# One buffer and one transfer for both parts of a weight tile, its rest made by VectorE, and six buffers for the norms

## The chip, the core and the metric

One core of a Trainium2 chip runs the whole kernel: TensorE (PE) multiplies, VectorE (DVE), ScalarE (ACT) and GpSimd (POOL) do the elementwise work, SyncE (SP) issues almost all transfers. The metric is the time of one execution in microseconds (us), as the median of several runs.

## The reference

One layer of a hybrid encoder over 2048 tokens of width 1024, in float32. What matters here is its first third, the input projection and the mixers that read it:

```python
h = rms_norm(x, mix_norm_g[l])
proj = h @ w_in[l]                      # (2048, 1024) @ (1024, 3332)
pa, pb, pc = ...                        # columns of A, B, C
# A: chunked attention, B: forgetting attention: q and k are RMS-normed per head of 64
# C: RWKV-7 recurrence over its columns (r, k, v and three low-rank inputs)
x = x + concat([ya, yb, yc]) @ w_out[l]
x = x + conv_glu_ffn(rms_norm(x, ffn_norm_g[l]), w_up[l], conv_w[l], conv_b[l], w_down[l])
```

## The kernel before

Tokens lie along the free axis. The first phase walks over four blocks of 512 tokens. For each block it makes the projection by tiles of weights (26 tiles of 1024 rows by 128 columns, or halves of that depth by 256 or 260), the q and k norms (`qk_in`), the v rows (`v_in`), and three interleaved stages of the recurrence: `rwkv_front`, `rwkv_inverse` (a chain of 62 small VectorE instructions, tiles `tm` and `T`) and `rwkv_back`. The later phases (attention, output projection, feed-forward) are not touched.

To keep float32 accuracy, each operand is split in two: a high part rounded to the matmul's type (`hi`, a ScalarE copy) and the rest (`lo`, a subtraction on another engine), and each product is three matmuls: hi by hi, hi by lo, lo by hi. In a projection these are lines 268 to 270; line 270 is the one that reads the weight's `lo`.

`load_w` delivers a weight tile. In the first block it loads the raw tile into `wraw` (three buffers), makes `whi` on ScalarE and `wlo` on GpSimd (on VectorE for five tiles: the first one and the four of `v_in`), two buffers of each, and stores both parts in DRAM with two transfers (`whiD`, `wloD`). In the three later blocks it reloads both parts with two transfers, in two of three cases into `whi` and `wlo`, in the third into two `wraw` buffers.

Small tiles of 128 by 512 with the tag `fl` come from one pool of four buffers in rotation: the squares `sq`, the scales `rn`, the split outputs `qh` and `ql` of the q and k norms, which are stored to DRAM (`qkD`), the sums `acc` of the norm of the next block, and a few more. A buffer is used again when all that read it, a store too, have ended.

The code asks for a weave of these jobs; the framework then sets the order of the instructions on each engine when the program is built, and adds the waits. Each engine takes its own instructions strictly in that order, SP's transfers too.

Of the kernel before, what the change touches and what calls it, by code (L numbers as in the profile page):

```python
# [11 lines left out]
F32 = mybir.dt.float32  # L12
F32R = mybir.dt.float32r
# [15 lines left out]
LEV = {'acc': G_, 'w': G_, 'kka': V, 'kf': V, 'rk': V, 'n': V, 'l': V, 'ql': V, 'ak': G_, 'gn': V, 'kr': V, 'uv': S_, 'r': V, 'w_': V, 'y': V, 'dt': V, 'bp': V, 'qa': V}  # L29
NEED = (21, 9, 4, 0, 9, 20, 6, 59)  # L30
AHEAD = 3
XG = 4
BUFS = {"fr": 7, "bk": 4, "bp": 2, "fl": 4, "wraw": 3, "wspl": 2, "xt": 2, "pr": 3, "p2": 6, "vs": 1, "st": 4, "raw": 3, "yh": 5, "xr": 3, "tmp": 5, "wu": 4, "s4": 4, "hid": 4, "x4": 3, "vv": 1}
PACE = 1
KSTAT = 1
X0N = 1
# [11 lines left out]
DQ = lambda nc: nc.sync  # L48
PSB = {"m": 3, "f": 2, "b": 2}
PSM = {"m": "PQVSNBLq", "f": "TA", "b": "b"}  # L50
WB = (2, 0)
GAP = ((0, 0, 21, 0), (12, 0, 12, 0), (12, 0, 3, 0), (15, 0, 0, 0))
PARK = 3
QQ = lambda nc: nc.scalar
# [43 lines left out]
def trunk_kernel(ctx: ExitStack, tc: tile.TileContext, xT, w_in, pp, cst, cau, rel, relr, w2, a2, g2, w_out, w_up, w_down, out, dbg=None):  # L98
    nc = tc.nc
# [3 lines left out]
    def f(ap):  # L103
        return ap.bitcast(F32)
# [4 lines left out]
    dram = ctx.enter_context(tc.tile_pool(name="dram", bufs=1, space=DRAM))  # L109
# [32 lines left out]
    def split(hi, lo, src, hi_eng=None, lo_eng=None):  # L142
        (hi_eng or nc.scalar).copy(hi, src) if (hi_eng or nc.scalar) is nc.scalar else hi_eng.tensor_copy(out=hi, in_=src)  # L143
        (lo_eng or nc.vector).tensor_tensor(lo, src, f(hi), op=ALU.subtract)  # L144


    p1 = ExitStack()
    hTp = p1.enter_context(tc.tile_pool(name="hTp", bufs=1, side="right"))
    xtp = p1.enter_context(tc.tile_pool(name="xtp", bufs=1, side="right"))
    ws = p1.enter_context(tc.tile_pool(name="ws", bufs=1, side="right"))  # L150
    wl = p1.enter_context(tc.tile_pool(name="wl", bufs=1, side="right"))
    flp = p1.enter_context(tc.tile_pool(name="flp", bufs=BUFS["fl"], side="right"))
    sp = p1.enter_context(tc.tile_pool(name="sp", bufs=4))
# [81 lines left out]
        nc.vector.memset(S, 0.0)  # L235
        Ss.append(S)

    kept, turn = {}, [0]

    def load_w(r0, c0, w, n, lo_eng=None, raw=None, who="Q"):  # L240


        src = w_in[r0 : r0 + n * P, c0 : c0 + w]
        if (r0, c0) in kept:
            turn[0] = (turn[0] + 1) % 3
            if turn[0] == 0:
# [6 lines left out]
        if raw is None:
            raw = wl.tile([P, n, 1040 // n], F32, name="wraw", tag="wraw", bufs=BUFS["wraw"])
            nc.sync.dma_start(out=raw[:, :, 0:w], in_=src.rearrange("(k p) c -> p k c", p=P))
        hi, lo = (ws.tile([P, n, 1040 // n], F32R, name=m, tag=m, bufs=2) for m in ("whi", "wlo"))
        split(hi[:, :, 0:w], lo[:, :, 0:w], raw[:, :, 0:w], None, lo_eng or LEV['w'](nc))
        kept[r0, c0] = [dram.tile([P, n, w], F32, name=f"{m}{r0}_{c0}") for m in ("whiD", "wloD")]
        for t, d in zip((hi, lo), kept[r0, c0]):
            nc.sync.dma_start(out=d, in_=f(t[:, :, 0:w]))  # L260
        return hi, lo

    def project(hT, c0, raw=None, who="P"):

        hi, lo = load_w(0, c0, P, KT, raw and nc.vector, raw, who)
        ps = psm[who].tile([P, TB], F32, name="mm", tag="ps")
        for kt in range(KT):
            mm(ps, hi[:, kt, 0:P], hT[kt][:, 0, :], start=(kt == 0), stop=False)  # L268
# [573 lines left out]
    for b in range(NB):  # L842
# [3 lines left out]
        lo = {} if b else lo0  # L846
# [25 lines left out]
    p2 = ExitStack()  # L872
# [245 lines left out]
    for u, (n, qb) in enumerate(units):  # L1118
# [8 lines left out]
        k = 0  # L1127
# [58 lines left out]
    for b, (t0, n) in enumerate(BL):  # L1186
        done = Y
        for hf in range(2):
# [11 lines left out]
            for k in range(KT):  # L1200
# [3 lines left out]
                yh = yhp.tile([P, 2, HN], F32R, name="yh")[:, :, 0:n]  # L1204
# [24 lines left out]
            for ct in range(KT):  # L1229
                xt = Y[ct][:, cs]  # L1230
# [19 lines left out]
    s4 = p4.enter_context(tc.tile_pool(name="s4", bufs=BUFS["s4"]))  # L1250
# [6 lines left out]
    x4 = p4.enter_context(tc.tile_pool(name="x4", bufs=BUFS["x4"]))  # L1257
# [206 lines left out]
```

## Time and profile before

| | |
|---|---|
| median of 3 runs | 3266.54 us (3254.4 to 3267.34) |
| the profiled execution, its time | 3256.01 us |
| its span from first to last instruction | 3254.2 us |
| first phase, blocks 1 to 4 | to 343, 630, 915 and 1195 us |

The profiled execution is one of the quicker ones: 10.5 us below the median of the runs. The ends of the blocks are read from the first reload of weights (342.9 us) and from the repeating pattern behind it, to a few us. A row of a timeline gives start, duration, engine, line, operation, output and inputs, the count of merged instructions, and in brackets the idle time of that engine just ahead and what ended it. A row of windows gives the stretch and its length, the busy time of TensorE, its weight loads, VectorE, ScalarE and GpSimd with their counts of instructions, then TensorE's granted clock, the busy share of the DMA engines and what they moved in GB/s. A row of waits gives who waited for whom, the sum, the count and the longest. The granted clock of TensorE is 1.00 at 2.4 GHz and 0.50 at 1.2 GHz.

### The profile page before, as it was taken

How to read it: one execution, taken by the hardware profiler on the slowest of the kernel's cores; microseconds unless marked ns; L12 is line 12 of the kernel's file. 1: busy time of each engine (PE TensorE's matmuls, PEld its weight loads, DVE VectorE, ACT ScalarE, POOL GpSimd, SP SyncE). 2: the span in 40 equal slices, each digit the busy share in tenths (PEclk: the TensorE clock that was granted, in tenths of full speed). 3: DMA queues.
4: the chain of work that ended last, by engine and by line, in shares of the span. 5: the costliest groups of instructions: out<-in, count | busy, mean ns of one | idle time of the engine just before them, and what ended most of it. 6: DMA issues, size and time to landing. Idle time of an engine off the chain costs nothing.

```text
span 3254.2 us, 49317 instructions
## 1 busy us (share of the span) xinstructions
PE 3037.6 (93%) x17820; PEld 2650.9 (81%) x17820; DVE 2373.9 (73%) x4569; ACT 1399.3 (43%) x2610; POOL 1000.3 (31%) x949
## 2 busy tenths in 40 slices
PE   6888899999999979999999999999899999999999
PEld 4567777776777755667699899999799998899999
DVE  5666666766677645677644688889988889988886
ACT  5343444434444334578733333333333334333332
POOL 3221001001000020144433444444544444444442
PEclk8888899999999987999999999999999999999999
DMA  7555665655653565532224422222422222422221
GB/s 222 148 166 170 175 181 163 190 149 157 162 161 101 169 152 141 141 99 77 76 90 148 143 79 78 78 78 74 154 74 77 78 78 81 140 78 78 78 79 67
DMA packets 440228, 392.94 MB, mean 121 GB/s; under 512 B 138809, under 2 KB 365637, under 8 KB 438633
## 3 DMA queue, kind: packets, MB, share of 16 engines
q1 hardware_dynamic: 435056, 377.99, 39.7%
q0 software_dynamic: 2816, 8.39, 0.9%
q10 hardware_dynamic: 2112, 3.41, 0.5%
q8 instruction: 141, 2.31, 0.3%
q14 instruction: 103, 0.84, 0.1%
HBM read 304.65 MB, written 86.36 MB: 120 GB/s over the span
## 4 chain that ended last, share of the span: by engine, by line
PE 66%; DVE 18%; issue 5%; ACT 4%; DMA 4%; POOL 2%; SPq 1%; POOLq 0%; ACTq 0%; DVEq 0%
PE ps L1291 7%; PE ps L1290 7%; PE ps L1289 7%; PE ps L1337 4%; PE ps L1335 4%; PE ps L1336 4%; PE mm L268 3%; PE mm L270 3%; PE mm L269 3%; DVE T L523 2%; PE o L1061 2%; DVE tm L520 2%; DVE wu L144 2%; PE z L639 2%; PE ps L1197 2%
## 5 line engine op out<-in xcount | busy, mean ns | idle before, releaser
L1291 PE MATMUL ps<-B,wu 128*128 128x340 f32 (+1 forms) x1848 | 593.2, 321 | 20.0 <-DVE wu L144 20.0
L1290 PE MATMUL ps<-B,wu 128*128 128x340 f32 (+1 forms) x1848 | 592.0, 320 | 0.0
L1289 PE MATMUL ps<-B,wu 128*128 128x340 f32 (+1 forms) x1848 | 589.4, 319 | 2.5 <-ACT wu L143 1.7
L1291 PEld LDWEIGHTS ps<-B,wu 128*128 128x128 f32 x1848 | 348.0, 188 | 27.6 <-DVE wu L144 27.2
L1335 PE MATMUL ps<-hid,wd 128*128 128x340 f32 (+1 forms) x1056 | 342.1, 324 | 14.3 <-ACT wd L143 10.2
L1289 PEld LDWEIGHTS ps<-B,wu 128*128 128x128 f32 x1848 | 347.9, 188 | 3.2 <-ACT wu L143 2.0
L1290 PEld LDWEIGHTS ps<-B,wu 128*128 128x128 f32 x1848 | 348.6, 189 | 0.1
L1337 PE MATMUL ps<-hid,wd 128*128 128x340 f32 (+1 forms) x1056 | 339.9, 323 | 3.1 <-POOL wd L144 3.0
L1336 PE MATMUL ps<-hid,wd 128*128 128x340 f32 (+1 forms) x1056 | 339.9, 322 | 0.0
L144 DVE TENSOR_TENSOR wu<-S,wu 128x512 fp32r<-128x512 f32 x264 | 257.0, 978 | 74.7 <-ACT wu L143 74.7
L1338 DVE TENSOR_TENSOR acc<-acc,ps 128x340 f32<-128x340 f32 (+1 forms) x528 | 248.3, 503 | 52.9 <-PE ps L1337 52.2
L144 POOL TENSOR_TENSOR wd<-raw,wd 128x1024 fp32r<-128x1024 f32 x66 | 171.0, 2613 | 277.3 <-ACT wd L143 272.9
L268 PE MATMUL mm<-hT,whi 128*128 128x512 f32 x520 | 235.9, 454 | 18.0 <-ACT whi L143 12.8
L270 PE MATMUL mm<-hT,wlo 128*128 128x512 f32 x520 | 220.3, 424 | 10.4 <-POOL wlo L144 6.4
L143 ACT CAST wu<-S 128x512 fp32r<-128x512 f32 x264 | 163.1, 619 | 150.5 <-PE ps L1291 137.9
L269 PE MATMUL mm<-hT,whi 128*128 128x512 f32 x520 | 219.3, 422 | 4.9 <-DVE hT L144 3.9
L1335 PEld LDWEIGHTS ps<-hid,wd 128*128 128x128 f32 x1056 | 201.8, 191 | 18.0 <-ACT wd L143 11.0
L144 DVE TENSOR_TENSOR wu<-raw,wu 128x512 fp32r<-128x512 f32 x198 | 203.0, 1026 | 6.4 <-ACT wu L143 6.4
L1337 PEld LDWEIGHTS ps<-hid,wd 128*128 128x128 f32 x1056 | 200.2, 190 | 5.5 <-POOL wd L144 5.5
L1336 PEld LDWEIGHTS ps<-hid,wd 128*128 128x128 f32 x1056 | 201.2, 190 | 0.0
L143 ACT CAST wu<-raw 128x512 fp32r<-128x512 f32 x198 | 121.5, 620 | 165.3 <-PE ps L1291 147.4
L268 PEld LDWEIGHTS mm<-hT,whi 128*128 128x128 f32 x520 | 105.5, 203 | 49.5 <-ACT whi L143 13.6
(348 smaller groups left out, 7140.4 us busy)
## 6 DMA issues: line engine op xcount, KB each, us to landing
raw<-in_w_up_dram SPq DMA_DIRECT2D x132, 512.0 KB
raw<-in_w_down_dram SPq DMA_DIRECT2D x66, 512.0 KB
whi<-whiD SPq DMA_DIRECT2D x48, 512.0 KB
wlo<-wloD SPq DMA_DIRECT2D x48, 512.0 KB
wraw<-in_w_in_dram SPq DMA_DIRECT2D x24, 512.0 KB
whiD<-whi SPq DMA_DIRECT2D x24, 512.0 KB
wloD<-wlo SPq DMA_DIRECT2D x24, 512.0 KB
xt<-in_xT_dram SPq DMA_DIRECT2D x48, 256.0 KB
```

Source lines behind the costliest of these rows:

```text
L143: (hi_eng or nc.scalar).copy(hi, src) if (hi_eng or nc.scalar) is nc.scalar else hi_eng.tensor_copy(out=hi, in_=src)
L144: (lo_eng or nc.vector).tensor_tensor(lo, src, f(hi), op=ALU.subtract)
L268: mm(ps, hi[:, kt, 0:P], hT[kt][:, 0, :], start=(kt == 0), stop=False)
L269: mm(ps, hi[:, kt, 0:P], hT[kt][:, 1, :], start=False, stop=False)
L270: mm(ps, lo[:, kt, 0:P], hT[kt][:, 0, :], start=False, stop=(kt == KT - 1))
L1289: mm(ps, whl[:, 0, kt, :], Bs[p][:, kt, 0, 0:n], start=(kt == 0), stop=False)
L1290: mm(ps, whl[:, 0, kt, :], Bs[p][:, kt, 1, 0:n], start=False, stop=False)
L1291: mm(ps, whl[:, 1, kt, :], Bs[p][:, kt, 0, 0:n], start=False, stop=(kt == 3))
L1335: mm(ps, wd[:, 0, ch], hid[:, 0, cs], start=(u == 0), stop=False)
L1336: mm(ps, wd[:, 0, ch], hid[:, 1, cs], start=False, stop=False)
L1337: mm(ps, wd[:, 1, ch], hid[:, 0, cs], start=False, stop=(u == G - 1))
L1338: nc.vector.tensor_tensor(acc[ct][:, cs], acc[ct][:, cs], ps, op=ALU.add)
```

## The change

`load_w` now takes one buffer for both parts (`pair`, three buffers), stores it with one transfer in the first block and reloads it with one in the later blocks. The rest `lo` is made by VectorE for all 26 tiles. `wraw` has two buffers instead of three and serves only the first block's loads. The pool `fl` has six buffers instead of four. The scratch of GpSimd's own transfers is set to 8192 bytes.

```diff
-BUFS = {"fr": 7, "bk": 4, "bp": 2, "fl": 4, "wraw": 3, "wspl": 2, "xt": 2, ...}
+BUFS = {"fr": 7, "bk": 4, "bp": 2, "fl": 6, "wraw": 2, "w": 3, "xt": 2, ...}
...
-    kept, turn = {}, [0]
-    def load_w(r0, c0, w, n, lo_eng=None, raw=None, who="Q"):
-        src = w_in[r0 : r0 + n * P, c0 : c0 + w]
+    kept = {}
+    def pair(n):
+        return wl.tile([P, 2, n, 1040 // n], F32R, name="w", tag="w", bufs=BUFS["w"])
+    def load_w(r0, c0, w, n, raw=None):
+        t = pair(n)
         if (r0, c0) in kept:
-            turn[0] = (turn[0] + 1) % 3
-            if turn[0] == 0:
-                hl = [wl.tile([P, n, 1040 // n], F32R, name="wraw", ...) for _ in range(2)]
-            else:
-                hl = [ws.tile([P, n, 1040 // n], F32R, name=m, tag=m, bufs=2) for m in ("whi", "wlo")]
-            for t, d in zip(hl, kept[r0, c0]):
-                nc.sync.dma_start(out=f(t[:, :, 0:w]), in_=d)
-            return hl
...
-        split(hi[:, :, 0:w], lo[:, :, 0:w], raw[:, :, 0:w], None, lo_eng or LEV['w'](nc))
-        kept[r0, c0] = [dram.tile([P, n, w], F32, name=f"{m}{r0}_{c0}") for m in ("whiD", "wloD")]
-        for t, d in zip((hi, lo), kept[r0, c0]):
-            nc.sync.dma_start(out=d, in_=f(t[:, :, 0:w]))
-        return hi, lo
+            nc.sync.dma_start(out=f(t[:, :, :, 0:w]), in_=kept[r0, c0])
+        else:
+            if raw is None:
+                raw = wl.tile([P, n, 1040 // n], F32, name="wraw", tag="wraw", bufs=BUFS["wraw"])
+                nc.sync.dma_start(out=raw[:, :, 0:w], in_=w_in[...])
+            split(t[:, 0, :, 0:w], t[:, 1, :, 0:w], raw[:, :, 0:w], None, nc.vector)
+            kept[r0, c0] = dram.tile([P, 2, n, w], F32, name=f"wD{r0}_{c0}")
+            nc.sync.dma_start(out=kept[r0, c0], in_=f(t[:, :, :, 0:w]))
+        return t[:, 0], t[:, 1]
...
-    nc = _bacc.Bacc("TRN2", target_bir_lowering=False, num_devices=1)
+    nc = _bacc.Bacc("TRN2", target_bir_lowering=False, num_devices=1, dynamic_dma_scratch_size=8192)
```

The change also moves instructions, since the framework orders the whole first phase anew (lines behind the edit stand 7 lower in the new file, so L679 and L672 are one line of code). Three places follow. The first is ScalarE in the first block at the second and third q norm that are made inside the recurrence (`sq`, then `rn`, `qh`); in brackets is what a row waits for. Before:

```order
L143 CAST qh_1067<-rn_1063 128x512 [waits DVE_49]
L143 CAST whi_1209<-wraw_1207 128x8x128 [waits DMAHW4_49,DMAHW6_49,PE_49,Pool_49]
L679 ACTIVATE sq_1088<-mm_1051 128x512 [waits PE_49]
L684 ACTIVATE rn_1112<-mm_1110,eps_63 128x512 [waits DVE_49,PE_49]
L685 ACTIVATE rn_1112<-rn_1112 128x512 [waits Activation_49]
L143 CAST qh_1116<-rn_1112 128x512 [waits DVE_49]
L143 CAST whi_1287<-wraw_1285 128x8x128 [waits DMAHW5_49,DMAHW7_49,PE_49,Pool_49]
L679 ACTIVATE sq_1137<-mm_1100 128x512 [waits DVE_49,PE_49]
```

The same place now:

```order
L142 CAST qh_1028<-rn_1024 128x512 [waits DVE_49]
L672 ACTIVATE sq_1049<-mm_1012 128x512 [waits PE_49]
L677 ACTIVATE rn_1070<-mm_1068,eps_63 128x512 [waits PE_49]
L678 ACTIVATE rn_1070<-rn_1070 128x512 [waits Activation_49]
L142 CAST qh_1074<-rn_1070 128x512 [waits DVE_49]
L142 CAST w_1240<-wraw_1241 128x8x128 [waits DMAHW4_49,DMAHW0_49]
L672 ACTIVATE sq_1095<-mm_1058 128x512 [waits PE_49]
```

The last `sq` no longer waits for VectorE, and the splits into `w` no longer wait for TensorE and GpSimd.

The second place is VectorE where the first head pair of the recurrence makes `AK`, the input of TensorE's line 454 (now 447). Before:

```order
L417 TENSOR_SCALAR rn<-mm 128x512
L283 SCALAR_TENSOR_TENSOR r<-mm,pps,r 128x511
L284 SCALAR_TENSOR_TENSOR r<-carry,pps,r 128x1
L287 COPY carry<-mm 128x1
L436 TENSOR_TENSOR KR_170<-r,E 128x512
L421 SCALAR_TENSOR_TENSOR rn<-k,pps,rn 128x512
L423 TENSOR_TENSOR kka<-rn,a 128x512
L431 TENSOR_TENSOR KR_170<-rn,E 128x512
L425 TENSOR_SCALAR a<-a,pps,oka 128x512
L426 TENSOR_TENSOR a<-a,k 128x512
L434 TENSOR_TENSOR AK<-a,sigw 128x4x128
```

The same place now:

```order
L280 COPY carry<-mm 128x1
L429 TENSOR_TENSOR KR_167<-r,E 128x512
L143 TENSOR_TENSOR w<-wraw,w 128x8x128
L414 SCALAR_TENSOR_TENSOR rn<-k,pps,rn 128x512
L416 TENSOR_TENSOR kka<-rn,a 128x512
L424 TENSOR_TENSOR KR_167<-rn,E 128x512
L418 TENSOR_SCALAR a<-a,pps,oka 128x512
L419 TENSOR_TENSOR a<-a,k 128x512
L276 SCALAR_TENSOR_TENSOR v<-mm,pps,v 128x511
L427 TENSOR_TENSOR AK<-a,sigw 128x4x128
```

The subtraction of a weight tile (L143) and one step of `v` (L276) now stand ahead of `AK` on VectorE; GpSimd's queue lost its 21 subtractions.

The third place is ScalarE at the start, where `rsb` is the scale of the first block's norm. Before:

```order
L143 CAST whi_273<-wraw_271 128x8x128 [waits DMAHW1_49]
L143 CAST whi_375<-wraw_373 128x8x128 [waits DMAHW7_49,DMAHW2_49,PE_49]
L143 CAST whi_412<-wraw_410 128x8x128 [waits DMAHW3_49,DMAHW4_49,PE_49,Pool_49]
L323 ACTIVATE rsb_308<-mm_306,eps_63 128x512 [waits PE_49]
L324 ACTIVATE rsb_308<-rsb_308 128x512 [waits Activation_49]
L143 CAST hT0_319<-x0_120 128x512 [waits DVE_49]
```

The same place now:

```order
L142 CAST w_265<-wraw_266 128x8x128 [waits DMAHW0_49]
L142 CAST w_364<-wraw_365 128x8x128 [waits DMAHW1_49]
L316 ACTIVATE rsb_299<-mm_297,eps_63 128x512 [waits DVE_49,PE_49]
L317 ACTIVATE rsb_299<-rsb_299 128x512 [waits Activation_49]
L142 CAST hT0_310<-x0_117 128x512 [waits DVE_49]
L142 CAST w_398<-wraw_399 128x8x128 [waits DMAHW7_49,DMAHW6_49]
```

The third split now stands behind `rsb`.

## Rows read from the trace of the kernel before

**Rows 1.** The page: busy time, share of the span and instructions of each engine.

```profile
PE 3037.6 (93%) x17820; PEld 2650.9 (81%) x17820; DVE 2373.9 (73%) x4569; ACT 1399.3 (43%) x2610; POOL 1000.3 (31%) x949
```

**Rows 2.** Windows of the first two blocks.

```profile
0.00:343.00 343.00, 272.77 (x1367) 207.03 (x1367) 209.68 (x477) 150.76 (x273) 81.30 (x73) 0.86 0.61 176
343.00:630.00 287.00, 266.09 (x1543) 209.40 (x1543) 183.76 (x524) 120.88 (x255) 26.25 (x43) 0.93 0.64 174
```

**Rows 3.** Waits of TensorE in the first block: who for whom, us, times, longest.

```profile
PE mm L268 <- ACT whi L143: 12.8, 4, 7.5
PE mm L682 <- ACT sq L679: 11.3, 3, 6.5
PE mm L270 <- POOL wlo L144: 6.4, 5, 1.7
...
PE rw L454 <- DVE AK L434: 4.8, 1, 4.8
...
PE rw L454 <- DVE T L523: 2.6, 1, 2.6
```

**Rows 4.** Waits of TensorE in blocks 2 to 4.

```profile
PE z L639 <- DVE S L643: 16.4, 12, 5.3
...
PE mm L270 <- DMA wlo<-wloD: 3.9, 3, 2.4
```

**Rows 5.** Timeline of TensorE, the longest idle stretch behind the start.

```profile
150.93 2.08 PE L682 MATMUL mm<-sq,cst 128*128 128x512 f32 x2 [6.47 <-ACT sq L679]
```

**Rows 6.** Timeline of ScalarE, the instruction that ends that stretch.

```profile
150.28 0.60 ACT L679 ACTIVATE sq<-mm 128x512 f32<-128x512 f32 x1 [4.93 <-DVE ql L144]
```

**Rows 7.** Timeline of VectorE ahead of it.

```profile
139.20 0.17 DVE L520 TENSOR_TENSOR tm<-T,NT 128x16 f32<-128x16 f32 x1
139.40 2.38 DVE L523 TENSOR_TENSOR T<-T,tm 128x16 f32<-128x16 f32 x1
...
147.34 2.84 DVE L144 TENSOR_TENSOR ql<-rn,qh 128x512 fp32r<-128x512 f32 x1 [4.20 <-DMA qkD<-qh]
```

**Rows 8.** Timeline of SP's transfers ahead of it.

```profile
142.22 2.55 SPq L528 DMA_DIRECT2D iD<-T  x4
144.87 0.54 SPq L691 DMA_DIRECT2D qkD<-qh  x1
```

**Rows 9.** Timeline of GpSimd in the same stretch.

```profile
139.37 2.38 POOL L144 TENSOR_TENSOR wlo<-wraw,whi 128x1024 fp32r<-128x1024 f32 x1 [6.42 <-ACT whi L143]
...
147.29 2.35 POOL L144 TENSOR_TENSOR wlo<-wraw,whi 128x1024 fp32r<-128x1024 f32 x1
```

**Rows 10.** Windows of ten us around it.

```profile
150.00:160.00 10.00, 9.07 (x21) 5.59 (x22) 2.23 (x5) 4.76 (x9) 0.00 (x0) 0.50 0.19 44
```

**Rows 11.** The tile `wlo`: who makes it; ns, shortest/median/longest.

```profile
L144 POOL TENSOR_TENSOR wlo<-wraw,whi x21: 2348/2385/2429, 20.6 to 294.4; 128x1024 fp32r<-128x1024 f32 x21
L144 DVE TENSOR_TENSOR wlo<-wraw,whi x5: 1211/1227/1241, 7.5 to 306.5; 128x1024 fp32r<-128x1024 f32 x3, 128x1040 fp32r<-128x1040 f32 x2
```

**Rows 12.** Timeline of VectorE: three that overlap a `wlo`, and L426 without one.

```profile
58.83 1.67 DVE L144 TENSOR_TENSOR ql<-rn,qh 128x512 fp32r<-128x512 f32 x1 [0.68 <-ACT qh L143]
...
83.22 2.72 DVE L426 TENSOR_TENSOR a<-a,k 128x512 f32<-128x512 f32 x1
...
116.73 0.69 DVE L426 TENSOR_TENSOR a<-a,k 128x512 f32<-128x512 f32 x1
...
294.40 2.37 DVE L284 SCALAR_TENSOR_TENSOR r<-carry,pps,r 128x1 f32<-128x1 f32 x1
```

**Rows 13.** Timeline of ScalarE at the start.

```profile
31.02 1.05 ACT L143 CAST whi<-wraw 128x1024 fp32r<-128x1024 f32 x1 [8.67 <-PE mm L269]
32.07 0.69 ACT L323 ACTIVATE rsb<-mm,eps 128x512 f32<-128x512 f32 x1
```

**Rows 14.** Waits of SP in blocks 2 to 4.

```profile
SPq L251 <- PE mm L270: 111.7, 28, 8.8
```

**Rows 15.** The page: a reload, count and size of one transfer.

```profile
whi<-whiD SPq DMA_DIRECT2D x48, 512.0 KB
```

More of the change, by code (lines that the diff above doesn't have):

```diff
@@ L32 @@
 XG = 4
-BUFS = {"fr": 7, "bk": 4, "bp": 2, "fl": 4, "wraw": 3, "wspl": 2, "xt": 2, "pr": 3, "p2": 6, "vs": 1, "st": 4, "raw": 3, "yh": 5, "xr": 3, "tmp": 5, "wu": 4, "s4": 4, "hid": 4, "x4": 3, "vv": 1}
+BUFS = {"fr": 7, "bk": 4, "bp": 2, "fl": 6, "wraw": 2, "w": 3, "xt": 2, "pr": 3, "p2": 6, "vs": 1, "st": 4, "raw": 3, "yh": 5, "xr": 3, "tmp": 5, "wu": 4, "s4": 4, "hid": 4, "x4": 3, "vv": 1}
 PACE = 1
@@ L50 @@
 PSM = {"m": "PQVSNBLq", "f": "TA", "b": "b"}
-WB = (2, 0)
 GAP = ((0, 0, 21, 0), (12, 0, 12, 0), (12, 0, 3, 0), (15, 0, 0, 0))
@@ L149, in trunk_kernel @@
     xtp = p1.enter_context(tc.tile_pool(name="xtp", bufs=1, side="right"))
-    ws = p1.enter_context(tc.tile_pool(name="ws", bufs=1, side="right"))
     wl = p1.enter_context(tc.tile_pool(name="wl", bufs=1, side="right"))
@@ L236, in trunk_kernel @@
         Ss.append(S)
-    kept, turn = {}, [0]
-    def load_w(r0, c0, w, n, lo_eng=None, raw=None, who="Q"):
-        src = w_in[r0 : r0 + n * P, c0 : c0 + w]
-        if (r0, c0) in kept:
-            turn[0] = (turn[0] + 1) % 3
-            if turn[0] == 0:
-                hl = [wl.tile([P, n, 1040 // n], F32R, name="wraw", tag="wraw", bufs=BUFS["wraw"]) for _ in range(2)]
-            else:
-                hl = [ws.tile([P, n, 1040 // n], F32R, name=m, tag=m, bufs=2) for m in ("whi", "wlo")]
-            for t, d in zip(hl, kept[r0, c0]):
-                nc.sync.dma_start(out=f(t[:, :, 0:w]), in_=d)
-            return hl
[L253 to L256, printed above, removed]
-        split(hi[:, :, 0:w], lo[:, :, 0:w], raw[:, :, 0:w], None, lo_eng or LEV['w'](nc))
-        kept[r0, c0] = [dram.tile([P, n, w], F32, name=f"{m}{r0}_{c0}") for m in ("whiD", "wloD")]
-        for t, d in zip((hi, lo), kept[r0, c0]):
-            nc.sync.dma_start(out=d, in_=f(t[:, :, 0:w]))
-        return hi, lo
+    kept = {}
[3 more added lines that the diff above has]
+        t = pair(n)
+        if (r0, c0) in kept:
+            nc.sync.dma_start(out=f(t[:, :, :, 0:w]), in_=kept[r0, c0])
+        else:
+            if raw is None:
+                raw = wl.tile([P, n, 1040 // n], F32, name="wraw", tag="wraw", bufs=BUFS["wraw"])
+                nc.sync.dma_start(out=raw[:, :, 0:w], in_=w_in[r0 : r0 + n * P, c0 : c0 + w].rearrange("(k p) c -> p k c", p=P))
+            split(t[:, 0, :, 0:w], t[:, 1, :, 0:w], raw[:, :, 0:w], None, nc.vector)
+            kept[r0, c0] = dram.tile([P, 2, n, w], F32, name=f"wD{r0}_{c0}")
+            nc.sync.dma_start(out=kept[r0, c0], in_=f(t[:, :, :, 0:w]))
+        return t[:, 0], t[:, 1]
     def project(hT, c0, raw=None, who="P"):
-        hi, lo = load_w(0, c0, P, KT, raw and nc.vector, raw, who)
+        hi, lo = load_w(0, c0, P, KT, raw)
         ps = psm[who].tile([P, TB], F32, name="mm", tag="ps")
@@ L696, in v_in @@
         c0, n = ((512, 256), (1280, 260))[g]
-        whl = [load_w(hf * 512, c0, n, 4, nc.vector) for hf in range(2)]
+        whl = [load_w(hf * 512, c0, n, 4) for hf in range(2)]
         if g == 1:
```

## The prediction

> **What bounds the kernel now.** I began with the page's share of each engine: TensorE is busy for 93% of the span [rows 1], so a saving counts only where TensorE stands idle or runs at its lower clock. The change touches the first phase alone, so I looked at that by blocks [rows 2]. The second block takes 287 us and TensorE is busy for 266 of them; the first takes 343 us with TensorE busy for 273, idle for 70, at a mean clock of 0.86 against 0.93. The first block is also where weights are split, so it is where the change can earn most. Then I read whom TensorE waits for there [rows 3] and behind it [rows 4]. In the first block five rows stand out: ScalarE's splits, the squares of the norms, GpSimd's subtraction, and VectorE on its way to AK. Of the 12.8 us for the splits, 7.5 are the very first load, which stays. In blocks 2 to 4 the waits for the reloaded second part are only 3.9 us, and the longest sum there, 16.4 us, is the recurrence's own chain, which stays.
>
> **The third norm.** The longest idle stretch behind the start is 6.47 us, ahead of the norm's matmul [rows 5]. Read backwards: the square it needs began on ScalarE at 150.28 after waiting for a VectorE subtraction, ql, that used a buffer of the same pool [rows 6]. That ql waited 4.20 us for a store to end, and then took 2.84 us [rows 7]. The store was issued at 144.87, behind the four transfers of iD, which were issued from 142.22, when the chain on T was done [rows 8]: SP's queue is in order, and a store of the norms sat behind the inverse. With six buffers this square waits for TensorE alone, as the order of the changed kernel shows, and the ql ahead of it waits for no store. I take the whole 6.5 us. Behind the stretch the clock stood at 0.50 for ten us with TensorE busy for 9.1 of them [rows 10], right after the idle stretch; at full clock that work would take half. I take 4.5 us for it. Term: 11 us; bounds 4 (the stretch is partly filled by the next wait, the inverse's own result, and the clock falls anyway) and 11.
>
> **GpSimd's subtraction moves to VectorE.** One takes 2.385 us on GpSimd and 1.227 us on VectorE [rows 11], both measured here on the same shape. TensorE waited for it 6.4 us in five places [rows 3]; 1.16 us less each is 5.8. VectorE is busy for 61% of this block [rows 2], so the subtraction will not always start at once. I take 4 us; bounds 0 and 6.4.
>
> What does VectorE pay? Added up by instructions, 21 x 1.227 = 25.8 us of new work on the engine that makes the recurrence's operands. But the trace shows a return. A step of T that takes as long as its neighbour, 0.17 us, took 2.38 us from 139.40 to 141.78, and exactly then, 139.37 to 141.75, GpSimd ran a subtraction [rows 7, 9]; the ql of 2.84 us lies over the next one, 147.29 to 149.64. A sum on one column took 2.37 us [rows 12]. Sixteen of GpSimd's 21 subtractions hold a VectorE instruction so, the first at 58.83 and the last at 294.40 [rows 12]; the excess over the usual duration of the same instruction, added over the timeline, is 26 us. So VectorE's time in the block stays as it is: 0 us; bounds of the effect on the path from -5 (the new work meets a chain, the freed time does not) to +5.
>
> The Trainium skill (SBUF — State Buffer, section on the two separate sides) says that GpSimd and a VectorE instruction with two SBUF inputs take one port pair as an exclusive lock, whole instruction by whole instruction. By that rule the held time goes with GpSimd's work, as I have taken it; a sum that only adds instructions would charge VectorE 25.8 us more. The rule also says that the lock works both ways, so that VectorE's new work will hold GpSimd's.
>
> AK is the place where both meet. TensorE waited 4.8 and 2.6 us ahead of line 454 [rows 3], with VectorE's L426 taking 2.72 us under a subtraction on GpSimd [rows 12] where its next instance took 0.69. The order of the changed kernel puts one subtraction (1.23) and one step of v (0.74) ahead of AK and removes two us of holding there and one just before. I take 2 us for the two places; bounds -1 and 5.
>
> **Order and buffers on ScalarE.** At the start the third split waited 8.67 us for a buffer and then ran for 1.05 us ahead of rsb, which the whole block needs [rows 13]. It now stands behind rsb: 1 us. Where ScalarE's split waits for TensorE to free one of two buffers, three pairs remove the wait; of the 12.8 us, 5.3 are left in three places behind the first load [rows 3], most of them for the raw tile itself: 1 us; bounds 0 and 3.
>
> **What costs nothing.** `wraw` with two buffers: one raw tile can load while another is split, and what hides the load is TensorE's work on the tile before; without that cover a load shows with its 512 KB at 176 GB/s [rows 2, 15], 3 us. The smaller scratch serves GpSimd's few stores, all off the path. One transfer instead of two saves SP's issue, and SP isn't waited for.
>
> **Reloads.** In blocks 2 to 4 a tile now waits for one transfer of 1 MB instead of two of 512 KB [rows 15], and there are three places for tiles instead of three and a half. SP stood for 111.7 us with a reload at its head, waiting for TensorE to release a buffer [rows 14], so reloads start as early as buffers allow, and in 78 tiles TensorE waits three times for the second part, 3.9 us in all [rows 4]. Half a tile at the 174 GB/s of the second block [rows 2] takes 3 us. I let one tile more be late by that, less 1 us for what six buffers return: -2 us. Bounds -14 (five tiles late) and +8, the latter because the order of all four blocks is made anew and TensorE idles 21 us in the second block alone [rows 2].
>
> **The sum.** 11 + 4 + 0 + 2 + 1 + 1 - 2 = 17 us. From the profiled execution's 3256.0 that gives 3239; it lies 10.5 us under the median of the runs shown, 3266.5, from which it would be 3249.5. I forecast the middle, 3244 us. A measurement of this kernel tells about 0.5%, 16 us, from no change, so the likeliest sum lies at that line.
>
> **The rivals.**
> *The clock comes too.* The first block at the second's clock of 0.93 instead of 0.86 [rows 2] would gain another 7% of 343 us, 24 us, less the 4.5 counted: 3256 - 17 - 20 = 3219, or 3224 between the two bases. For it: each idle stretch removed may spare a fall. Against it: most stretches in that block stay (the first load, the block's split input, the recurrence).
> *The waits come back.* What TensorE gains at the norm it loses at the next in-order result: the inverse's transfers, or VectorE, whose queue now holds the subtraction behind a run of steps on T. Then only rsb, part of the norm and part of the subtraction stay, some 5 us: 3256 between the bases. For it: VectorE is already busy for 210 of the block's 343 us [rows 2]. Against it: its time does not grow.
> *The reload becomes the wait (slower).* TensorE's line 268 could start on hi while lo was under way; now it waits for the last byte of both. If a reload is late, it is late by 3 us more. To turn the gain of 19 us into a loss of 16 takes 35 us, 12 late tiles of 78. Against it: SP waits at the head for the buffer [rows 14], so the transfer has TensorE's work on the other two tiles to hide behind. At 15 late tiles the time would be 3256 - 19 + 45 = 3282.
> The Trainium skill (DMA: Bandwidth & Descriptors, section on the anatomy of one DMA) says that the semaphore fires only once the last byte has landed, and that a transfer costs about 2 us beside its bytes. The first half speaks for this rival; by the second, one transfer in place of two would be an estimated 2 us sooner complete than two in a row.
>
> **How the numbers follow.** Forecast (a gain of 10 to 28 us): 0.55, of which 0.31 is above 16 us. The clock comes too: 0.19. The waits come back (gain of -4 to 10): 0.18, no measurable change. Reloads: 0.08, slower. That makes faster 0.50, same 0.42, slower 0.08. The likeliest case alone spans 3256 - 28 to 3266.5 - 10, 3228 to 3256. The range reaches into the clock's case and through the returned waits: 3224 to 3265.
>
> **What would show it.** The wait of the norm's matmul (L682, now L675) for its square, 6.5 us, is gone, and the clock is up in the window behind it. The subtraction's rows have 26 on VectorE at 1.23 us and none on GpSimd, no T step of 2 us is left, and VectorE's busy time in the first block is within 10 us of 210. The first block ends 12 to 25 us earlier, and blocks 2 to 4 take within 6 us of their 287, 285 and 280. The forecast is wrong if TensorE's waits for `w` by DMA exceed 15 us, if the first block ends at 335 or later, or if it ends before 315.

## The result, and the profile after

The changed kernel takes 3231.34 us as the median of 4 runs (3229.36 to 3239.98), the kernel before 3260.95 us in its runs beside them: ratio 0.9913, 95% interval 0.9889 to 0.9937, some 28 us faster by the ratio and 30 by the medians. The profiled execution took 3230.11 us against 3256.01, so 25.9 us lie between the two traces.

**After, the page:** the engines' line, to be held against [rows 1].

```profile
PE 3022.8 (94%) x17820; PEld 2638.5 (82%) x17820; DVE 2369.2 (73%) x4590; ACT 1397.6 (43%) x2610; POOL 952.5 (30%) x928
```

VectorE got 21 instructions more and is busy for 4.7 us less. To see where the time went, the first phase is cut at the first reload of weights, 342.9 us before and 315.5 after, and then in stretches of equal length.

**After, windows of the four blocks and of the rest** (columns as in [rows 2], which has the first two of before).

```profile
0.00:316.00 316.00, 258.36 (x1381) 195.72 (x1381) 209.26 (x501) 150.99 (x277) 32.92 (x52) 0.91 0.68 191
316.00:603.00 287.00, 268.11 (x1593) 209.19 (x1594) 189.96 (x552) 125.73 (x264) 26.84 (x43) 0.97 0.63 180
603.00:888.00 285.00, 269.87 (x1639) 210.22 (x1638) 195.13 (x580) 133.59 (x280) 26.31 (x43) 0.99 0.59 167
888.00:1168.00 280.00, 260.95 (x1655) 204.51 (x1654) 175.91 (x537) 110.25 (x252) 21.89 (x41) 0.94 0.45 126
1168.00:3228.00 2060.00, 1965.51 (x11560) 1818.86 (x11558) 1598.92 (x2422) 877.07 (x1540) 844.53 (x750) 0.98 0.31 96
```

**Before, the same windows behind the first two blocks.**

```profile
630.00:915.00 285.00, 266.43 (x1635) 206.51 (x1633) 193.90 (x571) 130.36 (x274) 26.01 (x43) 0.98 0.60 167
915.00:1195.00 280.00, 264.83 (x1725) 207.63 (x1724) 185.66 (x579) 120.60 (x272) 21.71 (x41) 0.99 0.48 132
1195.00:3254.00 2059.00, 1967.49 (x11558) 1820.29 (x11556) 1600.92 (x2422) 876.71 (x1540) 844.99 (x750) 0.97 0.31 96
```

The rest behind the first phase takes 2060 us after and 2059 before with the same matmuls, so the three later blocks together take 852 us in both: after, the second runs ahead (1593 rows of matmuls instead of 1543) and the fourth gives it back (1655 instead of 1725, at a clock of 0.94 instead of 0.99). Stretches of equal length can't show what each block takes by itself. The first projection matmuls of blocks 2, 3 and 4 start at 348.2, 618.4 and 892.2 us before and at 323.6, 582.3 and 852.3 us after, and the last of block 4 at 1191.5 and 1164.6: by these the second block takes 11 us less, the third 4 less and the fourth 13 more. Why the fourth is longer was not followed up. In sum, all that is left of the gain at the end of the phase is what the first block gained, 27 us. There the two windows split it: TensorE is idle for 316 - 258.4 = 57.6 us instead of 343 - 272.8 = 70.2, 12.6 less, and busy for 14.4 us less on nearly the same work (1381 rows instead of 1367), at a mean granted clock of 0.91 instead of 0.86.

**After, waits of TensorE in the first block** (to be held against [rows 3]).

```profile
PE mm L261 <- ACT w L142: 15.3, 4, 7.7
PE mm L675 <- ACT sq L672: 7.1, 3, 5.3
...
PE mm L263 <- DVE w L143: 3.8, 4, 1.3
PE rw L447 <- DVE v L277: 3.2, 1, 3.2
...
PE rw L447 <- DVE tm L513: 1.7, 1, 1.7
```

Of the 6.47 us ahead of the third norm [rows 5] 1.32 are left; the longest wait of a norm is now 5.35 us, at the block's second norm, which stands ahead of the recurrence's and waited 3.93 us before.

**After, TensorE's timeline at these two norms, and ScalarE's ahead of the first of them.**

```profile
58.06 2.08 PE L675 MATMUL mm<-sq,cst 128*128 128x512 f32 x2 [5.35 <-ACT sq L672]
...
135.75 1.12 PE L675 MATMUL mm<-sq,cst 128*128 128x512 f32 x2 [1.32 <-ACT sq L672]
```

```profile
56.47 1.05 ACT L142 CAST w<-wraw 128x1024 fp32r<-128x1024 f32 x1 [1.15 <-DMA wraw<-in_w_in_dram]
57.42 0.59 ACT L672 ACTIVATE sq<-mm 128x512 f32<-128x512 f32 x1
```

A split that waited 1.15 us for its raw tile stands ahead of the square. SP issued the loads there from 47.7 us on, where before it issued them from 35.1: this fits two raw buffers in place of three, though SP's order is new as well.

**After, the tile `w` and the tile `T` up to 316 us** (who works on it: ns, shortest/median/longest, first to last start).

```profile
L143 DVE TENSOR_TENSOR w<-wraw,w x26: 1212/1222/1237, 7.7 to 291.1; 128x1024 fp32r<-128x1024 f32 x24, 128x1040 fp32r<-128x1040 f32 x2
```

```profile
L513 DVE TENSOR_TENSOR tm<-T,NT x96: 132/212/1300, 107.2 to 315.8; 128x60 f32<-128x60 f32 x9, 128x28 f32<-128x28 f32 x6, 128x54 f32<-128x54 f32 x6, 128x48 f32<-128x48 f32 x6
...
L521 SPq DMA_DIRECT2D iD<-T x12: 558/588/1862, 132.9 to 272.5; - x12
```

**Before, the tile `T` up to 343 us.**

```profile
L520 DVE TENSOR_TENSOR tm<-T,NT x96: 153/214/2428, 109.8 to 342.7; 128x60 f32<-128x60 f32 x9, 128x28 f32<-128x28 f32 x6, 128x54 f32<-128x54 f32 x6, 128x48 f32<-128x48 f32 x6
...
L528 SPq DMA_DIRECT2D iD<-T x12: 595/604/609, 142.2 to 295.8; - x12
```

These rows hold a measure that the experiments use. The inverse is one chain of small steps on VectorE, and its first instance runs from the first `tm` to the first issue of `iD`: 109.8 to 142.2, 32.4 us, before, and 107.2 to 132.9, 25.7 us, after. The median step is as short as it was (0.21 us); the longest fell from 2.43 to 1.30 us.

**After, waits in blocks 2 to 4** (to be held against [rows 4, 14]): TensorE's for its reloads, and SP's.

```profile
PE z L632 <- DVE S L636: 14.9, 14, 2.5
...
PE mm L261 <- DMA w<-wD: 3.6, 2, 2.3
```

```profile
SPq L246 <- PE mm L263: 120.2, 28, 13.3
```

TensorE's waits for the single transfer sum to 3.6 us in three blocks; for the second of two they were 3.9, and for the first 0.8.

### The profile page after: what moved, and what is told of

Same layout as the page of the kernel before. It is cut to its first block, busy times and chain, and to the rows that moved or that the text cites. A ratio compares the mean times of both kernels' runs of the same rounds, so it can differ in the third digit from the quotient of the medians.

```text
span 3228.3 us, 49120 instructions
## 1 busy us (share of the span) xinstructions
PE 3022.8 (94%) x17820; PEld 2638.5 (82%) x17820; DVE 2369.2 (73%) x4590; ACT 1397.6 (43%) x2610; POOL 952.5 (30%) x928
## 4 chain that ended last, share of the span: by engine, by line
PE 66%; DVE 18%; issue 5%; DMA 4%; ACT 4%; POOL 2%; SPq 0%; POOLq 0%; ACTq 0%; DVEq 0%
PE ps L1284 7%; PE ps L1283 7%; PE ps L1282 7%; PE ps L1330 4%; PE ps L1328 4%; PE ps L1329 4%; PE mm L263 3%; PE mm L261 3%; PE mm L262 3%; PE o L1054 2%; DVE T L516 2%; DVE tm L513 2%; PE z L632 1%; PE ps L1190 1%; PE ps L1189 1%
## 5 line engine op out<-in xcount | busy, mean ns | idle before, releaser
L261 PE MATMUL mm<-hT,w 128*128 128x512 f32 x704 | 312.6, 444 | 23.7 <-ACT w L142 15.3
L143 DVE TENSOR_TENSOR wu<-S,wu 128x512 fp32r<-128x512 f32 x264 | 256.2, 975 | 75.6 <-ACT wu L142 75.5
L262 PE MATMUL mm<-hT,w 128*128 128x512 f32 x704 | 289.6, 411 | 6.2 <-DVE hT L143 5.9
L263 PE MATMUL mm<-hT,w 128*128 128x512 f32 x704 | 289.4, 411 | 3.9 <-DVE w L143 3.8
L143 POOL TENSOR_TENSOR wd<-raw,wd 128x1024 fp32r<-128x1024 f32 x66 | 170.7, 2610 | 277.5 <-ACT wd L142 272.5
L143 DVE TENSOR_TENSOR wu<-raw,wu 128x512 fp32r<-128x512 f32 x198 | 203.3, 1028 | 5.6 <-ACT wu L142 5.6
L261 PEld LDWEIGHTS mm<-hT,w 128*128 128x128 f32 x704 | 137.8, 196 | 67.5 <-ACT w L142 16.7
```

## The experiments

Theory H: the gain comes from GpSimd's subtraction leaving, because each held a VectorE instruction for as long as it ran, and the held ones stand in chains that TensorE waits for. Theory B: it comes from the buffers, those of the norms above all, as the largest term of the sum had it. A third possibility is the new order of the instructions, which comes with every change of `load_w`. Twelve runs in three groups; the kernel before took 3261.1, 3261.6 and 3260.3 us beside them (23, 18 and 13 runs).

| run | median us | ratio to before, 95% | first reload, us | first inverse, us |
|---|---|---|---|---|
| (before) | 3261 | 1 | 342.9 | 32.4 |
| (after) | 3231.3 | 0.9913 (0.9889 to 0.9937) | 315.5 | 25.7 |
| e_fl | 3260.4 | 0.9988 (0.9974 to 1.0001) | 342.1 | 31.4 |
| e_nofl | 3230.4 | 0.9894 (0.9876 to 0.9912) | 313.8 | 25.7 |
| e_dve | 3231.5 | 0.9890 (0.9871 to 0.9908) | 313.4 | 28.9 |
| e_hold | 3259.5 | 1.0001 (0.9981 to 1.0022) | 341.9 | 32.4 |
| e_mset | 3240.1 | 0.9923 (0.9898 to 0.9949) | 315.7 | 26.0 |
| e_half | 3243.9 | 0.9935 (0.9911 to 0.9959) | 321.8 | 29.0 |
| e_nodve | 3272.9 | 1.0034 (1.0018 to 1.0050) | 345.5 | 28.4 |
| e_nd3 | 3247.6 | 0.9956 (0.9940 to 0.9972) | 328.8 | 29.8 |
| e_acc | 3216.5 | 0.9855 (0.9831 to 0.9878) | 265.6 (moved in the order) | 25.8 |
| e_accak | 3204.4 | 0.9818 (0.9794 to 0.9842) | 305.1 | 25.7 |
| e_all | 3202.2 | 0.9824 (0.9801 to 0.9847) | 301.6 | 25.8 |
| e_dveaccak | 3208.0 | 0.9835 (0.9812 to 0.9859) | 300.7 | 28.8 |

The last two columns are read from the tiles `w` (or `whi`) and `T` of each trace, as above. The inverse's time also counts other VectorE work that the order puts between its steps, so it compares strictly only where the order is one: after, e_hold, e_mset and e_half. In these four the orders of TensorE, VectorE and ScalarE are the same, instruction by instruction. The median and the ratio of e_mset are of five runs; a sixth, of 5907.5 us, is left out as far outside the others.

### Buffers or VectorE

e_fl is the kernel before with the norms' six buffers and the small scratch alone:

```diff
-"fl": 4
+"fl": 6
-nc = _bacc.Bacc("TRN2", target_bir_lowering=False, num_devices=1)
+nc = _bacc.Bacc("TRN2", target_bir_lowering=False, num_devices=1, dynamic_dma_scratch_size=8192)
```

> The kernel before with six buffers for the norms (and the smaller scratch, which makes room for them), nothing else; TensorE's order stays nearly the same. If the third norm's wait is what the prediction says, the 6.5 us of idle time ahead of its matmul and the ten us at the lower clock behind it go: 7 to 12 us faster than before (ratio 0.9965). If the waits come back at the inverse's result right behind it: 0 to 4 us. If the gain of the change is the new order alone: nothing.

**e_fl, window of the first block and waits of TensorE in it.**

```profile
0.00:343.00 343.00, 272.76 (x1368) 207.57 (x1368) 207.72 (x478) 150.06 (x273) 82.95 (x73) 0.86 0.61 176
```

```profile
PE rw L454 <- DVE AK L434: 8.0, 2, 4.8
PE mm L682 <- ACT sq L679: 6.7, 4, 3.9
```

The norms' waits are 4.6 us shorter, and the third norm's is 1.44 us instead of 6.47, but over the whole block TensorE is as busy, and at the same clock, as in [rows 2]. Where the gain went is seen in two stretches: from the second norm of the recurrence to the next matmul of line 414, and from there to the one after it.

**Before, then e_fl: windows of these two stretches.**

```profile
139.84:178.23 38.39, 31.92 (x175) 23.00 (x176) 15.76 (x40) 16.69 (x32) 6.27 (x8) 0.82 0.44 122
178.23:290.84 112.61, 91.31 (x490) 71.27 (x489) 72.14 (x184) 46.90 (x94) 26.46 (x21) 0.86 0.58 169
```

```profile
139.87:169.16 29.29, 27.05 (x175) 19.67 (x176) 13.70 (x40) 16.45 (x32) 6.31 (x8) 1.00 0.58 159
169.16:288.16 119.00, 95.48 (x483) 73.84 (x482) 73.27 (x186) 47.46 (x94) 29.87 (x22) 0.81 0.58 169
```

In the first stretch e_fl gains 9.1 us, idle time and clock together. In the second it loses 6.4 of them, at a lower clock and with 2.2 us more of idle time, and the first reload comes only 0.8 us earlier. Among the waits AK's grew from 4.8 to 8.0 us, by a second one at 298.6 us, far behind the norm; what brought the clock down was not isolated. Six buffers alone are worth nothing that can be measured: 0.7 us by the medians, by the interval 8 us at most. That is the second of the three expectations, only that the gain is lost over the 170 us that follow and not right behind the wait.

e_nofl is the changed kernel with `"fl": 4`.

> The changed kernel with four buffers for the norms again; TensorE's order stays the same as in the changed kernel. If the six buffers carry 11 us, the gain of 29 us falls to some 18 (ratio to before 0.9945). If the order and the three pairs carry the gain, it stays at 25 us or more.

Nothing is lost without the six buffers. e_dve is the kernel before, where VectorE makes all 26 rests; buffers and transfers stay:

```diff
-split(hi[:, :, 0:w], lo[:, :, 0:w], raw[:, :, 0:w], None, lo_eng or LEV['w'](nc))
+split(hi[:, :, 0:w], lo[:, :, 0:w], raw[:, :, 0:w], None, nc.vector)
```

> The kernel before with the rest of all 26 weight tiles made by VectorE, nothing else. By the prediction's terms, 4 us for the waits for the subtraction and 2 for AK: 6 us faster (ratio 0.998), VectorE's busy time in the first block within 10 us of 210, and no step of the inverse of 2 us under a subtraction. If VectorE is charged all 25.8 us of new work, the first block gets longer by up to 10 us.

This one edit brings the whole gain, 29.6 us by the medians, far more than was expected of it; VectorE is busy for 207 us up to the first reload, within 10 us of 210 as expected. With four norm buffers the third norm's matmul waits for 1.39 us, not 6.47:

**e_dve, TensorE's timeline at the third norm, and SP's ahead of it.**

```profile
137.53 1.13 PE L682 MATMUL mm<-sq,cst 128*128 128x512 f32 x2 [1.39 <-ACT sq L679]
```

```profile
129.43 0.35 SPq L691 DMA_DIRECT2D qkD<-qh  x1
...
135.93 2.58 SPq L528 DMA_DIRECT2D iD<-T  x4
```

So the wait that showed on a buffer goes without more buffers. The chain on T ends 6 us earlier here than before (`iD` at 135.93 instead of 142.22), and in SP's new order the store of `qh` stands ahead of `iD` instead of behind it; this run doesn't tell which of the two removed the wait.

### Held, or something else that GpSimd does

e_hold is the changed kernel, in which GpSimd makes the 21 subtractions once more, into the raw tile that nobody reads again; what is computed stays, and so does every engine's order:

```diff
 split(t[:, 0, :, 0:w], t[:, 1, :, 0:w], raw[:, :, 0:w], None, nc.vector)
+if raw is not raw0 and n == KT:
+    nc.gpsimd.tensor_tensor(raw[:, :, 0:w], raw[:, :, 0:w], f(t[:, 0, :, 0:w]), op=ALU.subtract)
```

> The changed kernel, and GpSimd makes the same subtraction of 21 tiles a second time, into the raw buffer, whose values nobody reads afterwards; all orders stay. This doubles the suspected cost by itself: if a subtraction on GpSimd holds VectorE, VectorE's busy time in the first block rises by some 20 to 26 us and the first block by 5 to 12 us (ratio to before 0.994). If GpSimd's work costs nothing beside VectorE's, the time stays at that of the changed kernel (0.991); raw tiles held 3 us longer may cost up to 3 us in either case.

The whole gain is gone, though nobody reads what GpSimd makes there. VectorE is busy for 237 us in the first block, 28 more than in the changed kernel (20 to 26 had been expected), and the block is 26 us longer (5 to 12 had been expected). The inverse is back at 32.4 us. This run has the new order, the pairs, the six buffers and the rests made by VectorE: while GpSimd reads, all of them together, with VectorE's new work, leave the kernel where it was before.

**e_hold, window of its first block, then VectorE's and GpSimd's timelines in the first inverse.**

```profile
0.00:342.00 342.00, 269.45 (x1380) 202.53 (x1380) 237.43 (x499) 150.61 (x277) 85.57 (x73) 0.88 0.63 176
```

```profile
125.37 0.23 DVE L515 TENSOR_TENSOR tm<-T,NT 128x69 f32<-128x69 f32 x1
125.63 2.41 DVE L518 TENSOR_TENSOR T<-T,tm 128x69 f32<-128x69 f32 x1
```

```profile
125.59 2.37 POOL L253 TENSOR_TENSOR wraw<-wraw,w 128x1024 f32<-128x1024 f32 x1 [7.63 <-DVE tm L515]
```

This run also keeps the raw tile 2.4 us longer and GpSimd busier ahead of AK. e_mset does both as well but takes the reading away: zeros are written instead.

```diff
-    nc.gpsimd.tensor_tensor(raw[:, :, 0:w], raw[:, :, 0:w], f(t[:, 0, :, 0:w]), op=ALU.subtract)
+    for k in (KT, KT, 4):
+        nc.gpsimd.memset(raw[:, 0:k, 0:w], 0.0)
```

> The changed kernel, with GpSimd writing zeros three times (two whole tiles and a half, an estimated 2.4 us, from its memset of 128x1024 in 0.95 us) into the raw weight tile where the run that took the whole gain back let it subtract again (21 places, the same order on every engine; the raw tile is kept as long, GpSimd is as busy, and nothing that is computed changes). Theory 1, the gain is that VectorE's instructions are no longer held while GpSimd reads its two SBUF operands: GpSimd that only writes holds nothing, steps of T over it keep their 0.2 us, ratio to before 0.989 to 0.993 (3226 to 3240 us). Theory 2, the loss in that run came from the raw buffer that stays taken 2.4 us longer, or from GpSimd's queue ahead of AK and the sums of squares: ratio 0.997 to 1.002 here too, 3251 us or more.

**e_mset, GpSimd's timeline, then VectorE's in the same stretch.**

```profile
74.26 2.57 POOL L254 MEMSET wraw<- 128x1024 f32 x3 [11.57 <-DVE w L143]
77.45 1.98 POOL L254 MEMSET wraw<- 128x1024 f32 x2 [0.62 <-DVE w L143]
79.39 1.57 POOL L429 TENSOR_TENSOR AK<-kka,sigw 128x512 f32<-128x512 f32 x1
```

```profile
75.58 0.68 DVE L432 TENSOR_TENSOR KR<-r,E 128x512 f32<-128x512 f32 x1
76.18 1.22 DVE L143 TENSOR_TENSOR w<-wraw,w 128x1024 fp32r<-128x1024 f32 x1
77.31 0.74 DVE L417 SCALAR_TENSOR_TENSOR rn<-k,pps,rn 128x512 f32<-128x512 f32 x1
78.09 0.69 DVE L419 TENSOR_TENSOR kka<-rn,a 128x512 f32<-128x512 f32 x1
...
79.88 1.63 DVE L422 TENSOR_TENSOR a<-a,k 128x512 f32<-128x512 f32 x1
```

Under the writes the products with two inputs take their 0.68 to 0.69 us; under AK's product on GpSimd, which reads, one of the same size takes 1.63. e_mset keeps the gain, or nearly all of it. Between e_hold and e_mset lie 0.0078 of 3261 us, 25 us (19 by the medians; 15 to 36 by the two intervals), for one difference: whether GpSimd reads. What it reads includes the pair, which it so keeps longer, but in e_hold no engine waits for GpSimd to give back a pair; the raw tile is waited for in both.

**e_hold, then e_mset: waits of SP for GpSimd in the first 343 us, at the loads of raw tiles.**

```profile
SPq L250 <- POOL wraw L253: 10.5, 6, 3.4
```

```profile
SPq L250 <- POOL wraw L254: 12.8, 7, 2.7
```

H stands; the raw tile and GpSimd's queue can have caused no more than what is left between e_mset and the changed kernel, 3 us by the ratios and 9 by the medians.

The Trainium skill (SBUF — State Buffer, section on who interferes with whom) says that a VectorE instruction with two inputs in SBUF contends with a GpSimd instruction that reads SBUF, and not with one that only writes it. Both halves agree with these rows, for instructions with two inputs. Two small copies, with one input each, took longer beside memsets all the same:

**e_mset, VectorE's timeline beside memsets from 251.97 to 254.52 us.**

```profile
252.40 0.55 DVE L434 COPY EC<-E 64x8 f32<-64x8 f32 x1
252.96 1.00 DVE L435 COPY EC<-E 64x8 f32<-64x8 f32 x1
```

In the changed kernel each of the two takes 0.17 us there.

e_half is e_hold on half of each tile (`raw[:, 0:4, 0:w]`).

> The changed kernel, with GpSimd subtracting again on half of each raw tile (1024 columns become 512; about 1.3 us instead of 2.55, 21 places, the same order on every engine). Theory 1, what is lost is in proportion to the time that VectorE is held: half of the 28 us, ratio to before 0.9945 to 0.9975 (3243 to 3253 us), with 12 to 15 us of held time. Theory 2, the loss hangs on single places (one late chain that trips the clock): either nearly all of it (0.998 or more) or nearly nothing (0.993 or less).

The first inverse lands half way, 29.0 us between 25.7 and 32.4. The time loses 12.6 us by the medians and 7 by the ratios, of 28: a part, with an interval (0.9911 to 0.9959) that reaches from nothing to about half, so the time alone doesn't decide between the theories. The traces say more. Added up over the first block, one by one in the same order, VectorE's instructions are longer than in the changed kernel by 28.4 us in e_hold, 12.1 in e_half and 1.2 in e_mset, and the first reload comes 26.4, 6.3 and 0.2 us later. Between the first and the last step of the first inverse it is 6.6 us in e_hold and 3.2 in e_half: the whole of the 6.7 and 3.3 us by which that inverse is longer.

### What the pairs carry when GpSimd subtracts

e_nodve is the changed kernel with the 21 rests back on GpSimd (`lo_eng or LEV['w'](nc)`); e_nd3 has a third raw tile as well:

```diff
-"wraw": 2
+"wraw": 3
-dynamic_dma_scratch_size=8192
+dynamic_dma_scratch_size=4096
```

> The changed kernel with the 21 subtractions back on GpSimd; pair buffers, one transfer, two raw buffers, six norm buffers and the small scratch stay. Theory 1, only the move to VectorE counts: ratio to before 0.997 to 1.002, 3252 to 3268 us, steps of T of 2 us are back. Theory 2, the pairs or the single transfer carry a part of their own, 5 us or more: ratio 0.9985 or less with the first reload more than 5 us ahead of the kernel before.

> The changed kernel with the subtractions back on GpSimd (ratio 1.0034, slower than before) and a third raw buffer, made room for by a scratch of 4096 bytes. Theory 1, the 11 us by which that run was above the kernel before come from the raw tile: with two of them and a subtraction of 2.4 us the next load starts late, ScalarE's splits wait for it (10.3 us of idle instead of 4.5): ratio 0.998 to 1.001. Theory 2, they come from the pair buffer or the single store and reload: ratio stays at 1.002 to 1.005.

Both missed: e_nodve is slower than either theory had it, and the third raw tile brings more than twice the 11 us that its first theory gave it. Without the move to VectorE the rest of the change makes the kernel slower, by 0.0034, and a third raw tile, with the smaller scratch that makes room for it, then makes it faster by 25 us. The waits of TensorE in the first block say where:

**e_nodve.**

```profile
PE mm L261 <- ACT w L142: 16.7, 4, 7.8
...
PE mm L263 <- POOL w L143: 7.0, 3, 3.9
```

**e_nd3.**

```profile
PE mm L261 <- ACT w L142: 10.5, 2, 7.5
...
PE mm L263 <- POOL w L143: 2.8, 2, 1.5
```

With two raw tiles and a subtraction of 2.4 us the splits come late, 10.4 us more in these two waits. And e_nd3 is 0.0044 below the kernel before, so pairs, single transfer, six norm buffers or the new order are worth some 13 us while GpSimd subtracts; which of them is left open. With VectorE subtracting, neither shows: e_dve (no pairs, three raw tiles) and e_nofl (pairs, two raw tiles) stand at 0.9890 and 0.9894. The effects do not add up, and a third raw tile in the changed kernel itself wasn't tried.

### What still holds VectorE

In the changed kernel GpSimd still reads in the first phase, for the sums of squares (24 of 1.45 us) and AK (16 of 1.58 us). e_acc moves the first, e_accak both, e_all also the 16 additions of `yl` (15 in the changed kernel's trace, which can miss some); e_dveaccak does the same as e_accak on e_dve.

```diff
-LEV = {'acc': G_, ... 'ak': G_, ...}
+LEV = {'acc': V, ... 'ak': V, ...}
-        nc.gpsimd.tensor_tensor(yl, yl, bv, op=ALU.add)
+        nc.vector.tensor_tensor(yl, yl, bv, op=ALU.add)
```

(e_acc has the first entry alone; the last pair of lines is in e_all.)

> The changed kernel with two more of GpSimd's operations on VectorE: the sums of squares (24 x 1.45 us on GpSimd, 0.69 us on VectorE) and the first half of AK (16 x 1.58 us on GpSimd). They hold VectorE for about 31 us in the first four blocks (the excess over the usual duration of the same instructions), and would cost it 40 x 0.69 = 28 us. Theory 1, TensorE gains what is no longer held at the places where it waits for VectorE (some 12 us in the first block, less behind it): 3 to 15 us below the changed kernel, ratio to before 0.986 to 0.990. Theory 2, outside the first block TensorE hardly waits for VectorE, and its added work ahead of AK costs what the holding did: within 3 us of the changed kernel, 0.990 to 0.992; slower than the changed kernel by more than 3 us if VectorE's queue becomes the wait ahead of line 447.

> The changed kernel with only the sums of squares moved from GpSimd to VectorE (24 x 0.69 us there), AK's product left on GpSimd. The run with both moved was 27 us below the changed kernel. In the changed kernel's trace GpSimd's sums hold VectorE for 24.2 us of instructions in the first four blocks, AK's products for 5.4. Theory 1, what counts is held time: most of the 27 us, 18 to 27 (3204 to 3213, ratio to before 0.982 to 0.985). Theory 2, what counted was AK itself, 0.69 us instead of 1.58 us 16 times ahead of TensorE's line 447: at most 10 us (3221 or more, ratio 0.988 or more).

> The run with sums of squares and AK on VectorE, and yl's addition (15 x 1.31 us on GpSimd, an estimated 0.69 us on VectorE) as well. In the changed kernel yl holds VectorE for 1.1 us in all. Theory 1, held time: nothing left to gain, within 4 us of that run (ratio to before 0.981 to 0.983). Theory 2, any work that leaves GpSimd helps: 5 us or more below it. Theory 3, VectorE pays for 10 us of added work, and waits in its queue for bv's transfer: 5 us or more above it.

> The kernel before (two buffers and two transfers a tile, three raw buffers, four norm buffers) with all second parts, the sums of squares and AK on VectorE. Theory 1, buffers and transfers carry nothing: as the changed kernel with sums and AK moved, ratio to before 0.980 to 0.984. Theory 2, once VectorE is free of holding, the reloads or the norms' buffers show: 5 us or more above it, ratio 0.9835 or more.

e_accak gains another 27 us, more than either theory gave it. The sums alone bring 15 of these by the medians, 19 by the ratios. Held time demanded 18 or more and AK's own speed left 10 at most; e_acc's interval, 0.9831 to 0.9878, reaches into the first theory's range and ends just below the second's. So the larger part comes with the sums; what AK adds, 12 us by the medians and 0.0037 by the ratios, is hardly above the noise (intervals of 0.0024 to either side). `yl`, which held VectorE for 1.1 us, brings nothing. e_dveaccak is at the edge between its two theories, within the intervals of e_accak.

**e_accak, window of its first block.**

```profile
0.00:305.00 305.00, 253.83 (x1367) 194.46 (x1367) 201.16 (x511) 149.47 (x273) 11.07 (x38) 0.90 0.70 197
```

The sums and AK have gone over to VectorE, and it is busy for 201 us of that block, less than the changed kernel's 209; TensorE idles for 51 us. e_accak and e_all, at 3204 and 3202 us, are the best of all versions here.

## Why the prediction was right, and where not

The forecast, 3244 us, is 13 us above the 3231 measured, inside the likeliest case's own range and on the faster side. The sum of 17 us was measured as 27 in the first block. That it came so near is in part luck: the largest term, 11 of the 17, is worth nothing that can be measured, and the step put at 0, the holding of VectorE, is worth 19 to 25. Point by point:

- **The third norm, 11 us.** This is the step that failed. The wait was read rightly, and in its own stretch the term is there: 9.1 us in e_fl, idle time and clock together, with 1.44 us of the wait left. What failed is that the prediction carried it to the end of the block, where 0.8 us of it is left. That waits come back was named, as the term's lower bound of 4 and as a rival, but the term itself took the whole 11. Measured over the kernel it is worth nothing that stands out of the noise (e_fl 0.9988; e_nofl loses nothing).
- **GpSimd's subtraction to VectorE, 4 us, with VectorE at 0 and AK at 2.** Here lay the whole gain: 29.6 us by e_dve, 19 to 25 of them for the end of the holding alone (e_hold against e_mset). The 26 us of held instructions were read nearly rightly (a seventeenth subtraction, at 32.15 us, held a step of `x`), and VectorE's busy time stayed, 209.26 against 209.68. But they were set against the 25.8 us of new work as if only VectorE's load counted. The subtraction of a tile can wait behind a chain; a held step of T delays the whole chain: 6.7 us in the first inverse (e_hold against the changed kernel).
- **The clock, 4.5 us.** The idle terms of the sum, 6.5 + 4 + 2 + 1 + 1 = 14.5, came near the 12.6 us of idle time that went, by chance, since the 6.5 are the third norm's. The time that TensorE gained by its clock was 14.4, three times the term. The rival that the clock comes too was thus partly right: 0.91, where it took 0.93.
- **Order and buffers on ScalarE, 2 us.** Not seen: the waits for ScalarE's splits rose from 12.8 to 15.3 us, 5.3 with the first load left out before and 7.6 now. What `rsb` alone gained was not isolated.
- **`wraw` with two buffers, 0.** Not contradicted where VectorE subtracts (two in e_nofl, 0.9894; three in e_dve, 0.9890). With GpSimd subtracting the cover is gone and costs 25 us (e_nodve, e_nd3), as much as eight uncovered loads of the 3 us that were named.
- **Reloads, -2.** TensorE's waits for reloads were 3.6 us against 4.7 for both parts, a gain of 1 in place of a loss. The rival that the reload becomes the wait has nothing for it, and the 2 us that one transfer in place of two might save show in no wait of these runs.
- **The signs named in advance.** The 6.5 us wait down to 1.3, the clock up behind it (0.86 before, 1.00 after, in the window from 100 to 200 us), 26 subtractions on VectorE at 1.22 us, no step of T above 1.30 us, VectorE within 10 us of 210: as said. The first block ended 27 us earlier, above the 12 to 25, and its end at 315.5 lies half a us from the sign of being wrong at 315. Blocks 2 to 4 took their 852 us in sum, but by their first projections the second and the fourth are off by more than the 6 us allowed.

**After and before, the window from 100 to 200 us.**

```profile
100.00:200.00 100.00, 89.11 (x488) 65.54 (x487) 80.24 (x220) 47.29 (x88) 14.91 (x16) 1.00 0.67 182
```

```profile
100.00:200.00 100.00, 85.23 (x411) 62.86 (x409) 68.19 (x170) 38.30 (x67) 28.87 (x21) 0.86 0.55 155
```

In the same 100 us TensorE did 488 rows of matmuls instead of 411, with 15% more columns (the rows differ in size), and 5% more busy time.

## What to carry to other kernels

Where GpSimd and VectorE both read SBUF, look through VectorE's timeline for instructions that take as long as a GpSimd instruction beside them, and ask in which chain they stand: moving the GpSimd work to VectorE can cost nothing in busy time and shorten the chain, as it did here. An idle stretch that ends on a buffer is not yet an argument for more buffers; read on to what is late behind the buffer, try the buffers alone, and follow the gain to the end of the stage: here 9 us in the stretch itself were 0.8 us at the end of the block. And where a change removes idle time of TensorE, count the work done at the lower clock behind it as a term of its own, by the windows: here it was as large as the idle time.

## What was not expected of the hardware

That GpSimd's writes alone leave VectorE's instructions with two inputs as they are (63 memsets, 50 us more of GpSimd's time in the first 343 us, for a ratio of 0.9923 against 0.9913), while the same tiles, read, cost 19 to 25 us. Two copies of VectorE, of 64 by 8, did take 0.55 and 1.00 us beside memsets, where they take 0.17. And the holding goes the other way too: after the change a sum of squares on GpSimd in the first 345 us took a mean of 1637 ns where it had taken 1444, and the two longest, 2.27 and 2.33 us, each overlap one of VectorE's new subtractions of 1.2 us.
